# 96 short groups of unread TensorE products, at many operand distances, run behind the last product of an encoder kernel

## The chip, the cores and the metric

The kernel runs on one core of one Trainium2 chip. A core has TensorE (PE in the profile; PEld is its weight load), VectorE (DVE), ScalarE (ACT), GpSimd (POOL) and SyncE (SP), which work side by side and wait for each other through semaphores. A product reads two operands from SBUF, the stationary one (128 columns, loaded into the array first) and the moving one (256 or 512 columns streamed through it), and writes PSUM. The metric is the device time of one execution in microseconds, as a median over runs.

## The reference, cut to what matters

Two layers of an encoder on 256 tokens of width 2048, all in float32:

```
for i in range(DEPTH):                       # DEPTH = 2
    n = rms_norm(h, attn_norm[i])
    z = n @ w_in[i]                          # q, k, v and a query into 256 memory tokens
    h = h + concat([mix, cross]) @ w_o[i]    # neighbourhood attention in layer 0, grouped-query in layer 1
    n = rms_norm(h, mlp_norm[i])
    h = h + square(relu(n @ w_up[i])) @ w_down[i]   # 2048 -> 8192 -> 2048
return rms_norm(h, final_norm)
```

## The kernel before, in words

**Products.** Each float32 matrix is split into a rounded part and its remainder (`split`, lines 300 to 303: ScalarE makes "hi", VectorE "lo"), and each product is done as three TensorE products, hi by hi, hi by lo and lo by hi (`s_products` 216, `m_products` 203, `u_products` 729, `run` in `down_grains` 842). Where the weights stand still, 256 token columns move past them (lines 222 to 224 and 735 to 737); where the activations stand still, 512 weight columns move (lines 210 to 214 and 849 to 851). Attention has products of 256 columns too (365 to 367, 415 to 417).

**Stages.** The weights come chunk by chunk by DMA into rings of buffers; "grains" (class `Grain`, line 67) each load, split and multiply a half chunk, and `run_all` (247) goes through their list, starting loads and splits some grains ahead. The order is memory keys and values, layer 0 attention, output projection, MLP, then the same for layer 1. The MLP's down projection works by parts in a seven-product scheme (p1 to p7, `FIRST`, `SECOND`), whose shared sums stand in the tiles z0 and z1 and are folded into h (`folded`, 890), and its last part is done plainly (`plain_grains`, 903) in four column blocks of 512, 48 products each.

**The end.** The last block is done for one half of the tokens and then for the other. Line 945 runs the 24 products of a half and `finish` (1002) follows each half:

```
for i in range(NT):
    for n, (c, hf, k0, nk) in enumerate(PIECES):
        m_products(w, k0, nk, i, *own[c, hf], n == 0, n == 3, keep_order=True)
    w.done(w, i)
```

`finish` adds the scaled sum to h on VectorE (1006), sums squares on ScalarE (625, through `sum_squares`), reduces them on VectorE (1009, 309), takes the power on GpSimd (311), scales the row block on VectorE and ScalarE (1011, 1015, 1017) and starts four output transfers, two from ScalarE's queue and two from SyncE's (1020).

**Memory and order.** SBUF pools are stacked: "const", "keep" and "small" lie below, then "mlp" during the MLP, with z0 and z1 (8 KB a partition each), two buffers "c" (4 KB), six "a" (7 KB; the stationary activations of the down projection, line 794 and 800), and the split weights bh, bl, th, tl (their buffers serve h_p and l_p in the plain part). "side" lies at the other end. A pool that opens where another was closed waits tile by tile for what lies under it. Some operands are placed at offsets within their buffers, in bytes: `MOVING_AT` = 160, `STILL_AT` = 64 and the 480 in `wide("nT0", 480)` (lines 42 to 44, 185 to 187, 455 to 457, 739 to 741).

What one engine does comes in the order in which a planner found it ready, not in the order of the text, unless it is pinned. `pin` (line 189) keeps an instruction behind everything that the text has put on its engine so far. PSUM sums come from the pool "ps_acc", four buffers taken in turn; the last column block uses two of them.

Of the kernel before, what the change touches and what calls it, by code (L numbers as in the profile page):

```python
# [10 lines left out]
F32 = mybir.dt.float32  # L11
F32R = mybir.dt.float32r
# [5 lines left out]
P = 128  # L18
# [56 lines left out]
def encoder_kernel(ctx: ExitStack, tc: tile.TileContext, t: dict, out: bass.AP):  # L75
    nc = tc.nc
# [3 lines left out]
    def opened(name, side="left", space=None, bufs=1):  # L80
        kw = {"space": space} if space else {}
        manager = tc.tile_pool(name=name, bufs=bufs, side=side, reuse_waits="tile", **kw)
        pools[name] = manager, manager.__enter__()
        return pools[name][1]

    def closed(*names):
        for name in names:
            pools.pop(name)[0].__exit__(None, None, None)
# [57 lines left out]
    def halves_of(w):  # L146

        tiles = {}

        def load():  # L150
            tiles["raw"] = loaded(w.src, "U")

        def prep_early(hf):
            tiles[hf] = half_of_side(tiles["raw"], hf, MOVING_AT)

        def prep(hf):
            if hf == 0:
                tiles["raw"] = at.ring.tile([P, CH], F32, tag="raw", bufs=3, name="raw")
                nc.sync.dma_start(tiles["raw"], w.src)
            tiles[hf] = new_half(w.kind)  # L160
            split(*tiles[hf], tiles["raw"][:, hf * HALF : (hf + 1) * HALF])

        def run(hf):
            if hf == 0:
                w.start(w)
            hi, lo = tiles.pop(hf)
            if w.kind == "S":
                s_products(w, hf * (KT // 2), KT // 2, hi, lo)
            else:
                for i in range(NT):  # L170
                    m_products(w, w.first + 2 * hf, 2, i, hi, lo, w.begins and hf == 0, w.last and hf == 1)

        def after():
            if w.last:
                w.done(w)
            if w.early == "last":
                to_work()

        if w.early:
            return [Grain(lambda: run(0), None, load, None, lambda: prep_early(0), SOON),  # L180
                    Grain(lambda: run(1), after, None, None, lambda: prep_early(1), SOON)]
        return [Grain(lambda: run(0), None, None, None, lambda: prep(0)),
                Grain(lambda: run(1), after, None, None, lambda: prep(1))]
# [5 lines left out]
    pin = tc.keep_in_program_order  # L189

    def later(n, fn, *args):
        pending.append((state["tick"] + n, fn, args))

    def tick():
        state["tick"] += 1
        while True:
            due = [x for x in pending if x[0] <= state["tick"]]
            if not due:
                return
            pending.remove(due[0])  # L200
            due[0][1](*due[0][2])
# [24 lines left out]
    def begin():  # L226

        box["memT"] = at.cat.tile([P, KT, 512], F32R, tag="cat", name="memT")
        tiles = {}
        for w in plan[:FIRST_CHUNKS]:  # L230
            w.start(w)
        for q in range(4):
            for k in range(4 * q, 4 * q + 4):
                split_pair(box["memT"], mem0[:, k * SEQ : (k + 1) * SEQ], G_MEM, k)
                if k % 4 == 0:
                    for c, w in enumerate(plan[:FIRST_CHUNKS]):
                        if q % 2 == 0:
                            tiles[c] = new_half("S")
                        s = slice(q % 2 * 512, q % 2 * 512 + 512)
                        split(*(x[:, s] for x in tiles[c]), raws[c][:, q * 512 : (q + 1) * 512])  # L240
            for c, w in enumerate(plan[:FIRST_CHUNKS]):
                s = slice(q % 2 * 512, q % 2 * 512 + 512)
                s_products(w, 4 * q, 4, *(x[:, s] for x in tiles[c]))
        for w in plan[:FIRST_CHUNKS]:
            w.done(w)

    def run_all():
        begin()
        for w in plan[FIRST_CHUNKS:]:
            order.extend([w] if isinstance(w, Grain) else halves_of(w))  # L250
        reached = [0, 0, 0]

        def ahead(n):

            for stage in range(3):
                while reached[stage] < len(order) and reached[stage] < n + order[reached[stage]].ahead[stage]:
                    fn = order[reached[stage]].stages[stage]
                    reached[stage] += 1
                    if fn:
                        fn()  # L260

        for i in range(4):
            tick()
            ahead(min(i - 2, 0))
        for n, g in enumerate(order):
            ahead(n)
            g.run()
            if g.after:
                g.after()
            tick()  # L270
# [687 lines left out]
    def add_mlp(layer):  # L958
        for m in range(PK):
            plan.extend(up_grains(layer, 0, m))  # L960
        for x, (p, n) in enumerate(STEPS_OF):
            begins = x == 0 or HALF_OF[x - 1] != HALF_OF[x]
            ends = x == len(STEPS_OF) - 1 or HALF_OF[x + 1] != HALF_OF[x]
            up, down = up_grains(layer, p + 1, n), down_grains(layer, p, n, begins, ends)
            plan.extend((up[0], down[0], up[1], down[1]))
        for nb in range(4):
            plan.extend(plain_grains(layer, nb))
# [169 lines left out]
    add_o(1)  # L1137
    add_mlp(1)


    for j in range(8):
        later(3 + j, mem_squares, j)
# [4 lines left out]
        later(24 + j, x_norm, j)  # L1147
    later(26, x_stats)
    run_all()
    assert not pending, pending  # L1150
    closed(*reversed(list(pools)))

# [117 lines left out]
```

## Time and profile before

| what | us |
|---|---|
| median of two runs | 2051.15 |
| runs | 2050.47 and 2051.83 |
| the profiled execution, whole | 2048.73 |
| its span, first to last instruction | 2046.9 |
| TensorE busy | 2024.6 |
| VectorE busy | 1666.9 |
| ScalarE busy | 1242.6 |
| GpSimd busy | 126.4 |
| data read from HBM, in all | 401.32 MB, 200 GB/s over the span |

How to read it: times are counted from the first instruction. A line of the timeline has the start in us, the length in us, the engine, the line of the kernel, the operation, output and inputs by their names, the shapes, and how many records were merged; in brackets stands idle time just before it and what ended it. A line of the stretches has, for each engine, busy time and in brackets the records, then the granted TensorE clock, the share of the DMA engines and GB/s. A line of the groups has the count behind the x, then busy time in all and the mean of one in ns, then idle time and its releasers. A record of a product covers its whole way through the array, so records overlap; what a product takes from TensorE is the distance between two starts.

### The profile page before, as it was taken

How to read it: one execution, taken by the hardware profiler on the slowest of the kernel's cores; microseconds unless marked ns; L12 is line 12 of the kernel's file. 1: busy time of each engine (PE TensorE's matmuls, PEld its weight loads, DVE VectorE, ACT ScalarE, POOL GpSimd, SP SyncE). 2: the span in 40 equal slices, each digit the busy share in tenths (PEclk: the TensorE clock that was granted, in tenths of full speed). 3: DMA queues.
4: the chain of work that ended last, by engine and by line, in shares of the span. 5: the costliest groups of instructions: out<-in, count | busy, mean ns of one | idle time of the engine just before them, and what ended most of it. 6: DMA issues, size and time to landing. Idle time of an engine off the chain costs nothing.

```text
span 2046.9 us, 32742 instructions
## 1 busy us (share of the span) xinstructions
PE 2024.6 (99%) x13044; PEld 1832.8 (90%) x13044; DVE 1666.9 (81%) x2049; ACT 1242.6 (61%) x1628; POOL 126.4 (6%) x156
## 2 busy tenths in 40 slices
PE   8999999999999999999999999999999999999998
PEld 7899999889999999999988888889999999999996
DVE  6767677558998999989897667657989999999896
ACT  6645555456666666666656557556666666666664
POOL 0000000000000000010000001000000000000100
PEclk9999999999999999999999999999999999999999
DMA  7756666727777787777765544536777787777873
GB/s 281 281 193 208 217 211 213 288 77 237 228 229 232 217 241 230 221 233 231 225 211 216 178 170 146 200 114 229 233 231 231 220 240 217 232 226 221 243 222 131
DMA packets 101306, 440.16 MB, mean 215 GB/s; under 512 B 11424, under 2 KB 19232, under 8 KB 68000
## 3 DMA queue, kind: packets, MB, share of 16 engines
q1 hardware_dynamic: 82800, 402.40, 58.1%
q0 software_dynamic: 17776, 34.61, 9.1%
q8 instruction: 102, 1.67, 0.3%
q10 hardware_dynamic: 576, 1.05, 0.1%
q14 instruction: 52, 0.43, 0.1%
HBM read 401.32 MB, written 7.34 MB: 200 GB/s over the span
## 4 chain that ended last, share of the span: by engine, by line
PE 97%; DVE 1%; ACT 1%; issue 0%; DMA 0%; SPq 0%; POOLq 0%; POOL 0%; ACTq 0%
PE ps_u L737 11%; PE ps_u L735 11%; PE ps_u L736 11%; PE p L849 9%; PE p L850 9%; PE p L851 9%; PE ps_m L210 8%; PE ps_m L213 8%; PE ps_m L214 8%; PE ps_s L222 3%; PE ps_s L224 3%; PE ps_s L223 3%; PE pt_n L320 1%; DMA raw<-in_w_km 0%; PE pt_a L407 0%
## 5 line engine op out<-in xcount | busy, mean ns | idle before, releaser
L737 PE MATMUL ps_u<-hT,ul 128*128 128x256 f32 x2048 | 568.5, 278 | 1.8 <-DVE ul L303 1.8
L735 PE MATMUL ps_u<-hT,uh 128*128 128x256 f32 x2048 | 568.7, 278 | 0.0
L736 PE MATMUL ps_u<-hT,uh 128*128 128x256 f32 x2048 | 568.0, 278 | 0.0
L302 ACT ACTIVATE uh<-raw_U 128x1024 fp32r<-128x1024 f32 x278 | 294.7, 1061 | 313.9 <-PE ps_u L736 293.0
L735 PEld LDWEIGHTS ps_u<-hT,uh 128*128 128x128 f32 x2048 | 384.9, 188 | 5.5 <-ACT uh L302 0.3
L736 PEld LDWEIGHTS ps_u<-hT,uh 128*128 128x128 f32 x2048 | 384.8, 188 | 4.6
L737 PEld LDWEIGHTS ps_u<-hT,ul 128*128 128x128 f32 x2048 | 385.6, 188 | 3.7 <-DVE ul L303 2.6
L303 DVE TENSOR_TENSOR lo<-raw,hi 128x1024 fp32r<-128x1024 f32 (+1 forms) x224 | 266.3, 1194 | 148.0 <-ACT hi L302 145.9
L303 DVE TENSOR_TENSOR ul<-raw_U,uh 128x1024 fp32r<-128x1024 f32 x278 | 337.7, 1219 | 41.8 <-ACT uh L302 41.7
L302 ACT ACTIVATE hi<-raw 128x1024 fp32r<-128x1024 f32 (+1 forms) x224 | 231.7, 1040 | 204.4 <-PE ps_m L214 112.5
L302 ACT ACTIVATE th<-t 128x2048 fp32r<-128x2048 f32 x112 | 215.1, 1921 | 123.7 <-PE p L851 121.5
L303 DVE TENSOR_TENSOR tl<-t,th 128x2048 fp32r<-128x2048 f32 x112 | 256.2, 2287 | 36.5 <-ACT th L302 36.1
L303 DVE TENSOR_TENSOR bl<-b,bh 128x1536 fp32r<-128x1536 f32 x112 | 196.1, 1751 | 0.3 <-ACT bh L302 0.3
L850 PE MATMUL p<-tl,a_s 128*128 128x512 f32 x448 | 177.2, 395 | 0.0
L851 PE MATMUL p<-th,a_s 128*128 128x512 f32 x448 | 174.4, 389 | 0.0
L302 ACT ACTIVATE bh<-b 128x1536 fp32r<-128x1536 f32 x112 | 166.2, 1484 | 10.0 <-PE p L851 4.0
L829 POOL DMA_DIRECT2D t<-b x112 | 96.4, 861 | 1165.1 <-DVE t L828 506.7
L849 PE MATMUL p<-th,a_s 128*128 128x512 f32 x448 | 166.1, 395 | 0.0
L851 PE MATMUL p<-bh,a_s 128*128 128x512 f32 x336 | 131.1, 390 | 0.0
L850 PE MATMUL p<-bl,a_s 128*128 128x512 f32 x336 | 130.9, 390 | 0.0
L224 PE MATMUL ps_s<-nT,lo 128*128 128x256 f32 x448 | 125.4, 280 | 0.0
L222 PE MATMUL ps_s<-nT,hi 128*128 128x256 f32 x448 | 125.2, 279 | 0.0
(237 smaller groups left out, 3771.1 us busy)
## 6 DMA issues: line engine op xcount, KB each, us to landing
raw_U<-in_w_up SPq DMA_DIRECT2D x128, 1024.0 KB, 6.4
b<-in_w_pair SPq DMA_DIRECT2D x112, 768.0 KB, 4.5
raw<-in_w_o SPq DMA_DIRECT2D x32, 1024.0 KB, 5.0
t<-in_w_pair SPq DMA_DIRECT2D x112, 256.0 KB, 3.3
t<-b POOLq DMA_DIRECT2D x112, 256.0 KB, 6.8
raw<-in_w_b SPq DMA_DIRECT2D x21, 1024.0 KB, 5.0
raw<-in_w_av SPq DMA_DIRECT2D x12, 1024.0 KB, 5.0
raw<-in_w_aq SPq DMA_DIRECT2D x12, 1024.0 KB, 5.0
```

Of the source, the lines that this page charges most:

```text
L210: first = nc.tensor.matmul(w.ps[i], ah, hi[:, s], start=st, stop=False)
L213: nc.tensor.matmul(w.ps[i], ah, lo[:, s], start=False, stop=False)
L222: nc.tensor.matmul(ps, hi[:, s], acts[:, k, :SEQ], start=k == 0, stop=False)
L224: nc.tensor.matmul(ps, lo[:, s], acts[:, k, :SEQ], start=False, stop=k == KT - 1)
L302: first = nc.scalar.activation(dst_hi, src, AF.Copy)
L303: return first, nc.vector.tensor_tensor(dst_lo, src, dst_hi.bitcast(F32), op=ALU.subtract)
L735: nc.tensor.matmul(ps, hi[:, s], acts[:, k, :SEQ], start=k == 0, stop=False)
L736: nc.tensor.matmul(ps, hi[:, s], acts[:, k, SEQ:], start=False, stop=False)
L737: nc.tensor.matmul(ps, lo[:, s], acts[:, k, :SEQ], start=False, stop=k == KT - 1)
L849: nc.tensor.matmul(ps, a[:, 0, ai, :], hi[:, s], start=begins, stop=False)
L850: nc.tensor.matmul(ps, a[:, 0, ai, :], lo[:, s], start=False, stop=False)
L851: nc.tensor.matmul(ps, a[:, 1, ai, :], hi[:, s], start=False, stop=ends)
```

## The change

A function `unread_products` is added after line 1138 and called right after `run_all()`, so that its instructions come behind the whole program in the text. It closes the pool "mlp" and opens "idle" in its place, with two tiles that are filled with ones: "small_room" (640 columns, by GpSimd) and "room" (9344 columns, by VectorE). It takes one PSUM buffer of the pool "ps_acc", into which all its products go; nothing reads it. Every product is pinned.

First come 60 products of 512 columns from "small_room". Then 64 groups `narrow(x, e)`: two products of 512 columns, then fifteen of 256, in threes with the pattern of lines 735 to 737. Then 32 groups `wide_ones(y, z)`: two products of 256 columns, then twelve of 512, in threes with the pattern of lines 849 to 851. `piece` shifts an operand by `place % 256` bytes within "room", in steps of 32 bytes. As weights are loaded one product ahead, the distance that counts here is from a moving operand to the next stationary one: in a narrow group it is x inside, and e from the last entry product to the first of the fifteen; in a wide group y inside and z at the entry. That is eight distances inside, and eight (narrow) or four (wide) at the entry.

```diff
+    def unread_products():
+
+        closed("mlp")
+        idle = opened("idle")
+        small_room = idle.tile([P, 640], F32R, name="small_room")
+        nc.gpsimd.memset(small_room.bitcast(F32), 1.0)
+        room = idle.tile([P, 9344], F32R, name="room")
+        nc.vector.memset(room.bitcast(F32), 1.0)
+        ps = at.acc.tile([P, 512], F32, tag="acc", name="ps_x")
+
+        def product(still, moving, start, stop):
+            n = moving.shape[-1]
+            pin(nc.tensor.matmul(ps[:, :n], still, moving, start=start, stop=stop))
+
+        for n in range(60):
+            product(small_room[:, 512:640], small_room[:, :512], n == 0, n == 59)
+
+        def piece(first, place, n):
+            first += place % 256 // 4
+            return room[:, first : first + n]
+
+        def features(k, lo):
+            return piece(512 * k + 256 * lo, 0, 256)
+
+        def narrow(x, e):
+            for n in range(2):
+                product(piece(7424, 0, P), piece(4096 + 512 * n, x - e, 512), n == 0, n == 1)
+            for k in range(5):
+                hi, lo = (piece(f + 128 * k, x, P) for f in (2560, 3328))
+                product(hi, features(k, 0), k == 0, False)
+                product(hi, features(k, 1), False, False)
+                product(lo, features(k, 0), False, k == 4)
+
+        def wide_ones(y, z):
+            for n in range(2):
+                product(piece(2560, y, P), features(n, 0), n == 0, n == 1)
+            for k in range(4):
+                hi, lo = (piece(f + 128 * k, z, P) for f in (7424, 8320))
+                bh, bl = (piece(f + 512 * (k % 3), z - y, 512) for f in (4096, 5760))
+                product(hi, bh, k == 0, False)
+                product(hi, bl, False, False)
+                product(lo, bh, False, k == 3)
+
+        for x in range(0, 256, 32):
+            for e in range(0, 256, 32):
+                narrow(x, e)
+        for y in range(0, 256, 32):
+            for z in range(0, 256, 64):
+                wide_ones(y, z)
...
     run_all()
+    unread_products()
```

## The prediction, made before the change was run

> **What bounds the kernel now.** I read the page first, for the span and for whether anything but TensorE could carry the end.
>
> ```profile
> span 2046.9 us, 32742 instructions
> PE 2024.6 (99%) x13044; PEld 1832.8 (90%) x13044; DVE 1666.9 (81%) x2049; ACT 1242.6 (61%) x1628; POOL 126.4 (6%) x156
> PEclk9999999999999999999999999999999999999999
> ...
> PE 97%; DVE 1%; ACT 1%; issue 0%; DMA 0%; SPq 0%; POOLq 0%; POOL 0%; ACTq 0%
> ```
>
> TensorE is busy 99% of the span and makes 97% of the chain that ended last, at the full granted clock. So products that are added to its stream add their own time, unless they can be placed where TensorE stands still. The next view is the end of the run in order of time, because the change puts its work there: TensorE, then VectorE, then the other engines and the output.
>
> ```profile
> 2036.80 0.39 PE L213 MATMUL ps_m<-l_p,a_p 128*128 128x512 f32 x1
> ...
> 2037.70 0.39 PE L214 MATMUL ps_m<-h_p,a_p 128*128 128x512 f32 x1
> 2038.13 0.75 DVE L1006 SCALAR_TENSOR_TENSOR h<-ps_m,inv,h 128x512 f32<-128x512 f32 x1 [1.66 <-PE ps_m L214]
> 2040.09 0.55 POOL L311 TENSOR_TENSOR fin_r<-fin_v,mhalf 128x1 f32<-128x1 f32 x1 [4.80 <-DVE fin_v L309]
> 2041.35 0.48 DVE L1015 TENSOR_SCALAR h<-h,fin_r 128x512 f32<-128x512 f32 x1
> 2041.43 0.95 ACTq L1020 DMA_DIRECT2D out<-h  x2
> 2041.46 0.81 SPq L1020 DMA_DIRECT2D out<-h  x2
> ```
>
> The last product starts at 2037.70. Everything behind it, the final normalisation and the output transfers, takes until 2046.9. TensorE is therefore free for 9.2 us at the end and nowhere else.
>
> **How fast a product follows the one before.** The record of a product (0.28 us at 256 columns, 0.39 at 512) holds its passage through the array and overlaps the next, so the price is the distance from start to start. I took it from four stretches of the timeline. The rows are the first and the last of each.
>
> ```profile
> 136.41 0.28 PE L415 MATMUL av<-pT,vm 128*128 128x256 f32 x1
> ...
> 137.49 0.28 PE L365 MATMUL sc_ps<-km,qmT 128*128 128x256 f32 x1
> ...
> 952.22 0.28 PE L737 MATMUL ps_u<-hT,ul 128*128 128x256 f32 x1
> ...
> 957.52 0.28 PE L737 MATMUL ps_u<-hT,ul 128*128 128x256 f32 x1
> ...
> 1003.62 0.28 PE L735 MATMUL ps_u<-hT,uh 128*128 128x256 f32 x1
> ...
> 1004.22 0.28 PE L737 MATMUL ps_u<-hT,ul 128*128 128x256 f32 x1
> 1004.33 0.28 PE L735 MATMUL ps_u<-hT,uh 128*128 128x256 f32 x1
> ...
> 1008.98 0.28 PE L737 MATMUL ps_u<-hT,ul 128*128 128x256 f32 x1
> 1009.10 0.40 PE L849 MATMUL p<-th,a_s 128*128 128x512 f32 x1
> 1009.33 0.40 PE L850 MATMUL p<-tl,a_s 128*128 128x512 f32 x1
> 1009.57 0.39 PE L851 MATMUL p<-th,a_s 128*128 128x512 f32 x1
> ...
> 1011.88 0.39 PE L849 MATMUL p<-bh,a_s 128*128 128x512 f32 x1
> ```
>
> At 256 columns there are two steady rates for the same product with nothing else changed: 41 steps in 1008.98 - 1004.33 = 4.65 us, or 113.3 ns, and 45 steps in 957.52 - 952.22 = 5.30 us, or 117.8 ns. After a change of product the quick stretch first pays: five steps in 1004.22 - 1003.62 = 0.60 us, or 120 ns each. A short group, the nine steps from 136.41 to 137.49, never becomes quick: 1.08 us, or 120 ns each. At 512 columns, the four steps from 2036.80 to 2037.70 give 226 to 227 ns, which is twice 113.3 = 226.7; the twelve from 1009.10 to 1011.88 give 2.78 us, or 231.7 ns, with a worst single step of 0.24 us (1009.33 to 1009.57). No row is quicker than 113.3 and 226.7 at the full clock. So the place of the operands, or how a group was entered, costs 0 to 13 ns a product. The profile has no addresses, so I can't price each distance of the change by itself, only bound all of them by these rows.
>
> **The change, part by part.** It removes nothing and moves nothing; no DMA is issued, so no queue of SP, ACT or POOL gets longer by a transfer.
>
> Pool and buffers. The pool "mlp" is closed and "idle" opened at its start. Its 2.5 and 36.5 KB a partition lie over z0, z1, both c and the first two and a little of the third of the six buffers "a", by the sizes in the code. z0 was last read in the fold, 192 products of line 210 to 214 earlier; the "a" buffers are read by the last products.
>
> The two memsets. GpSimd fills 640 columns. The nearest rows are its own fills at the start:
>
> ```profile
> L130 POOL MEMSET ones<- 128x128 f32 x1 | 0.2, 205 | 0.3 <-POOLq L1260 0.3
> L132 POOL MEMSET mhalf<- 128x8 f32 x1 | 0.1, 105 | 0.0
> ...
> POOL fin_r L311 <- DVE fin_v L309: 61.5, 2, 56.7
> ```
>
> They give 100 ns for 120 more columns, so 640 columns take about 0.63 us. GpSimd waits idle for 56.7 us ahead of the first L311, and z0 is free by then, so I take nothing for it. If it is queued behind the second L311 (end 2040.64), TensorE would start at 2041.3 and not 2037.93: 3.3 us. Nothing that matters stands behind it on GpSimd but that L311.
>
> VectorE fills 9344 columns. The row L1015 (0.48 us for 512 columns) scaled up gives 8.8 us, L1006 (0.75 us) gives 13.7; without a fixed part it could be half of the first. It must wait for the readers of its part of "a" (the last of them six products ahead of the end), and what is queued behind it on VectorE is the final normalisation, so the output transfers may be 9 us later; their cover is 240 us of products. Its own cover is the first 60 products, 13.6 us from 2037.93, so until 2051.5. Even behind the whole normalisation (end 2041.83) it is done at 2050.6. At 13.7 us it would be 4.0 us late. I take nothing, which is the nearest row's answer.
>
> The products. 60 + 64 x 17 + 32 x 14 = 1596, of which 64 x 15 + 32 x 2 = 1024 have 256 columns and 60 + 64 x 2 + 32 x 12 = 572 have 512. They are pinned one behind the other and behind the last real product, they write one PSUM bank in order, and nothing reads it, so no wait lies between them. Quick bound: 1024 x 113.3 + 572 x 226.7 = 116.05 + 129.65 = 245.7 us. Dear bound: 1024 x 124 (the worst single step inside that 0.60 us, if the other four took 119) + 512 x 240 + 60 x 226.7 = 263.5 us. What I take: at 256 columns the groups have fifteen products, so a group that becomes quick still pays its first five, (5 x 120 + 10 x 113.3) / 15 = 115.5; a slow one 117.8; one like the short group 120. The middle is 117.8: 120.6 us. At 512, the groups have twelve; half of them at 226.7 and half at 231.7 is 229.2: 512 x 229.2 = 117.35 us. The 60 of the first stretch have the operands at equal places, as in a row with one rate all through, so 226.7: 13.6 us. Sum 251.55 us.
>
> The Trainium skill ("TensorE: Matmul & The Clock Gate", section "Step-by-step: what each phase is for") says that TensorE reads weights and the moving operand through two independent SBUF ports, so that loading the next weights takes nothing from the running product. By it distances would cost nothing and the sum would be the quick one; the 113.3 and 117.8 above, for one kind of product, speak against it. Section "Back-to-back issue gap" of the same page has N / 2.4 + 2.5 ns, 109.2 and 215.8; by that the products would take an estimated 235.2 us; the rows above, at 113.3 and 226.7, disagree.
>
> The end. The last record starts one step ahead of the sum's end: 2037.70 + 0.23 + 251.55 - 0.23 = 2289.25, and ends 0.39 later, 2289.64. Then the end of the program. In before, the last transfers are issued by 2042.4 and land 3.0 to 3.2 us after their issue, which leaves 1.3 to 1.8 us to 2046.9:
>
> ```profile
> out<-h ACTq DMA_DIRECT2D x4, 256.0 KB, 3.2
> out<-h SPq DMA_DIRECT2D x4, 256.0 KB, 3.0
> ```
>
> Part of this is the checking of those landings, which is over long before; I take 1.2. Span 2290.8. The execution lasted 2048.73, 1.83 beyond its span, so 2292.7; the median of the runs, 2051.15, is 2.42 above the profiled one, so a median of 2295.1, which I forecast as 2295.0 us: +11.9%.
>
> **The rivals.** (1) Distances cost nothing: all at the quick rate. For it, most long stretches are quick; against it, the groups here are short and their entries change on purpose. 251.55 falls to 245.7: 2289.
>
> (2) Some distance is cheaper than any in before, so that the quick rate isn't the floor. At the very start, at half the clock, a step is 0.213 us:
>
> ```profile
> 6.39 0.58 PE L222 MATMUL ps_s<-memT,hi 128*128 128x256 f32 x1 [6.39 <-ACT hi L302]
> ...
> 7.68 0.41 PE L224 MATMUL ps_s<-memT,lo 128*128 128x256 f32 x1
> ...
> 10.88 0.37 PE L224 MATMUL ps_s<-memT,lo 128*128 128x256 f32 x1
> 11.09 0.28 PE L222 MATMUL ps_s<-memT,hi 128*128 128x256 f32 x1
> ```
>
> Fifteen steps in 3.20 us, half of which is 106.7 ns. All 2168 units of 256 columns at 106.7 would be 231.3 us: 2275. Against it: no step in before comes near. (By the gap formula of the Trainium skill, on the page "TensorE: Matmul & The Clock Gate", named above, it would be an estimated 2279.)
>
> (3) Some distances clash worse than any in before. Price up to the dear bound: 263.5, so 2307. For it: before has few distances, fixed in its code; against it: the clashes that it has end within five steps or stay at 5 ns.
>
> (4) TensorE stands still at the entry, for one of the two fills: 3.3 or 4.0 us, or both late.
>
> ```profile
> 2038.10:2042.00 3.90, 0.00 (x0) 0.00 (x0) 2.21 (x5) 2.04 (x4) 0.55 (x1) 1.00 0.40 150
> 2042.00:2046.90 4.90, 0.00 (x0) 0.00 (x0) 0.00 (x0) 0.02 (x1) 0.00 (x0) 0.50 0.56 214
> ```
>
> The granted clock falls to 0.50 about 3.9 us after the last product, so a wait of that length may also be followed by cold steps: the start ran cold from 6.39 to 11.09, 4.7 us, a loss of half of it, 2.4 us. Together 3 to 10 us, middle 5: 2300. Against it: the fills have 56.7 us of idle GpSimd and 13.6 us of products as cover.
>
> (5) The other side: not slower. The products have no reader; if they are left out of the program, or fall into the 9.2 us that TensorE is free at the end, the time stays 2051. Only about 40 of the 1596 fit there, since 9.2 us / 0.2267 is 40, so the point from which it decides is that they aren't issued at all. Against it: they are written as ordinary products into a held bank.
>
> **How the numbers follow.** Chances: the forecast 0.62, rival 1 0.12, rival 2 0.02, rival 3 0.12, rival 4 0.09, rival 5 0.03. The range goes from 2287 (rival 1 at the profiled execution's level, 2289.2 - 2.42) to 2307 (the dear bound) and holds the forecast, rivals 1 and 4 and half of 3. About 2% is what a measurement of this kernel can tell from no change, and every case but rival 5 lies over 10% above before: slower 0.97, same 0.03, faster 0.
>
> **What would show it right or wrong.** Right: 14640 products; the first added one follows the one at 2037.70 by 0.23 us; the added ones take 246 to 263 us with no idle time between; within a group of fifteen, starts lie 113 to 124 ns apart, and within one of twelve 226 to 240, differing from group to group; the output transfers end early, and the span ends 1 to 2 us behind the last product. Wrong: a gap behind the 60 products or ahead of them (rival 4), steps over 130 ns at 256 columns for whole groups (rival 3 and beyond my range), all steps alike (rival 1), steps under 113 (rival 2).

## The result, and the profile after

The change takes 2297.32 us, the median of two runs (2294.45 and 2300.19), against 2051.15: the ratio is 1.12, with a 95% interval from 1.1138 to 1.1262. Forecast were 2295.0 us, 2287 to 2307. The profiled execution is the longer of the two runs, 2300.19 us.

The page of the changed kernel, its head and its chain:

```profile
span 2298.4 us, 35936 instructions
...
PE 2280.7 (99%) x14640; PEld 2062.5 (90%) x14640; DVE 1674.1 (73%) x2050; ACT 1243.2 (54%) x1628; POOL 127.1 (6%) x157
...
PE ps_x L1152 11%; PE ps_u L737 9%; PE ps_u L735 9%; PE ps_u L736 9%; PE p L849 7%; PE p L850 7%; PE ps_m L210 7%; PE p L851 7%; PE ps_m L213 7%; PE ps_m L214 7%; PE ps_s L224 3%; PE ps_s L222 3%; PE ps_s L223 3%; DMA t<-in_w_pair 1%; DVE ul L303 1%
```

TensorE has 1596 products more and 256 us more of busy time; VectorE has gained 7.2 us, and ScalarE and GpSimd less than 1. The chain that ended last now closes with the added line, L1152, at 11%. The same place as before, the end of the real work, in order of time over TensorE, GpSimd and VectorE:

```profile
2043.68 0.39 PE L214 MATMUL ps_m<-h_p,a_p 128*128 128x512 f32 x1
2043.91 0.84 PE L1152 MATMUL ps_x<-small_room 128*128 128x512 f32 x3
...
2041.23 0.63 POOL L1145 MEMSET small_room<- 128x640 f32 x1
...
2044.11 0.75 DVE L1006 SCALAR_TENSOR_TENSOR h<-ps_m,inv,h 128x512 f32<-128x512 f32 x1 [1.65 <-PE ps_m L214]
2046.76 7.84 DVE L1147 MEMSET room<- 128x9344 f32 x1 [1.90 <-issue]
2054.52 0.10 DVE L1009 TENSOR_REDUCE ss_f<-ssq 128x1 f32<-128x4 f32 x1
```

The first added product follows the last real one by 0.23 us. The small fill ended at 2041.86, 2.05 us ahead of its need. The large one ended at 2054.60, 2.9 us ahead of the end of the 60 products at 2057.51, and it did push the final normalisation back (L1009 behind it), under the products. The three stretches of the added part (busy time and records by engine, then the granted clock):

```profile
2043.90:2057.50 13.60, 13.60 (x61) 11.26 (x60) 9.92 (x6) 2.06 (x4) 0.56 (x1) 1.00 0.16 61
2057.50:2200.60 143.10, 143.10 (x1089) 137.42 (x1088) 0.00 (x0) 0.00 (x0) 0.00 (x0) 1.00 0.02 7
2200.60:2297.50 96.90, 96.86 (x450) 79.54 (x448) 0.00 (x0) 0.00 (x0) 0.00 (x0) 1.00 0.00 1
```

TensorE is busy without a gap at the full clock: 13.6 us for the 60, 143.1 for the narrow groups, 96.7 for the wide ones with the last step (to 2297.07 + 0.23), 253.4 in all. Five groups, cut to their inner products and merged in a line each (start, length in all, records), show that their steps differ:

```profile
2096.45 1.41 PE L1152 MATMUL ps_x<-room 128*128 128x256 f32 x11
...
2109.65 1.46 PE L1152 MATMUL ps_x<-room 128*128 128x256 f32 x11
...
2154.56 1.48 PE L1152 MATMUL ps_x<-room 128*128 128x256 f32 x11
...
2204.31 2.21 PE L1152 MATMUL ps_x<-room 128*128 128x512 f32 x9
...
2267.58 2.51 PE L1152 MATMUL ps_x<-room 128*128 128x512 f32 x10
```

Less the last record's 0.28 or 0.39 us, over one step less than records: narrow (64, 32) 113 ns, (64, 224) 118, (160, 96) 120; wide (0, 64) 227, (160, 128) 236. The first two have their operands at the same places and differ by the entry alone.

### The profile page after: what moved, and what is told of

It is laid out like the page before. It is cut to its first block, busy times and chain, and to the rows that moved or that the text cites. A ratio compares the mean times of both kernels' runs of the same rounds, so it can differ in the third digit from the quotient of the medians.

```text
span 2298.4 us, 35936 instructions
## 1 busy us (share of the span) xinstructions
PE 2280.7 (99%) x14640; PEld 2062.5 (90%) x14640; DVE 1674.1 (73%) x2050; ACT 1243.2 (54%) x1628; POOL 127.1 (6%) x157
## 4 chain that ended last, share of the span: by engine, by line
PE 94%; DVE 3%; DMA 2%; issue 1%; ACT 1%; SPq 0%; DVEq 0%; ACTq 0%
PE ps_x L1152 11%; PE ps_u L737 9%; PE ps_u L735 9%; PE ps_u L736 9%; PE p L849 7%; PE p L850 7%; PE ps_m L210 7%; PE p L851 7%; PE ps_m L213 7%; PE ps_m L214 7%; PE ps_s L224 3%; PE ps_s L222 3%; PE ps_s L223 3%; DMA t<-in_w_pair 1%; DVE ul L303 1%
## 5 line engine op out<-in xcount | busy, mean ns | idle before, releaser
L1152 PE MATMUL ps_x<-room 128*128 128x256 f32 (+1 forms) x1536 | 239.9, 318 | 0.0
L1152 PEld LDWEIGHTS ps_x<-room 128*128 128x128 f32 x1536 | 217.2, 188 | 22.6
```

What stands on the lines that cost most here:

```text
L1152: pin(nc.tensor.matmul(ps[:, :n], still, moving, start=start, stop=stop))
```

## The experiments

**The change again, beside the kernel before.** Ahead of the added part the first profiled execution was 6 us later than the one of before (2043.68 against 2037.70 for the last real product).

> The change unaltered, beside runs of the kernel before on one chip. Theory (the added products take 253.2 us, as they did in the first profile, and of that first profile's time some 6 us were waits for transfers ahead of the added part): the added stretch is 253.2 us again to 0.1, the last real product starts near 2037 and not at 2043.7, and the time is 2293 to 2295 us. Rival (the waits ahead belong to the change): the last real product starts near 2043 again, and the time is 2297 to 2300 us.

Measured: 2293.57 us, ratio 1.119 (1.1175 to 1.1206). In its timeline the last real product starts earlier than in before:

```profile
2036.82 0.39 PE L214 MATMUL ps_m<-h_p,a_p 128*128 128x512 f32 x1
2037.05 0.39 PE L1152 MATMUL ps_x<-small_room 128*128 128x512 f32 x1
```

The view of the tile of the added sums has the first and the last start of the groups:

```profile
L1152 PE MATMUL ps_x<-room x1536: 274/282/406, 2050.7 to 2290.2; 128*128 128x256 f32 x128, 128*128 128x512 f32 x64
```

The added stretch, from the first added start to the last, is 253.16 us in both executions, and none of its steps differs by more than 1 ns. The 6 us belong to that one execution, not to the change: set product against product, it fell behind the second execution by 3.6 us in its first 72 us and by another 3.3 between 1870 and 1993 us, ahead of every added product. The theory holds in its times; what the lost time was spent on was not looked into.

**Quick places.** 

```diff
-                narrow(x, e)
+                narrow(64, 32)
...
-                wide_ones(y, z)
+                wide_ones(0, 64)
```

> All 64 narrow groups at distance 64 inside and 32 at the entry, all 32 wide ones at 0 and 64, so as many products of each width as in the change. Theory (the distance from a moving operand to the next stationary one sets the step): the added stretch, first added start to last, falls from 253.2 to 247.9 us (64 groups of 2.174 us and 32 of 2.975 us, as this pair of distances took in the change, and 13.6 us), the time by 5 us. Rival (distances cost nothing and the steps differ by where in the stream a group lies): 253 us, no change.

**Dear places.** The same with `narrow(160, 96)` and `wide_ones(160, 128)`.

> All narrow groups at 160 inside and 96 at the entry, all wide ones at 160 and 128. Theory: the added stretch rises to 255.5 us (64 groups of 2.252 us, 32 of 3.055 us, and 13.6 us), 7.6 us above the run with the quick places. Rival (distances cost nothing): 253 us, the same as the run with the quick places.

Measured, side by side: 2287.46 us (ratio 1.1164, 1.1147 to 1.118) and 2295.75 us (1.1204, 1.1187 to 1.1221), with as many products of each width. The same view, first with the quick places and then with the dear ones:

```profile
L1152 PE MATMUL ps_x<-room x1536: 276/276/399, 2050.3 to 2284.1; 128*128 128x256 f32 x128, 128*128 128x512 f32 x64
```

```profile
L1152 PE MATMUL ps_x<-room x1536: 276/283/403, 2050.6 to 2292.1; 128*128 128x256 f32 x128, 128*128 128x512 f32 x64
```

233.8 against 241.5 us, and with the 60 products 247.3 and 255.1 where 247.9 and 255.5 were expected. The places, inside and at the entry together, are worth 8 us; that distances cost nothing is refuted, and so is the rival that the steps go by where in the stream a group lies.

**No cover.** 

```diff
-        for n in range(60):
-            product(small_room[:, 512:640], small_room[:, :512], n == 0, n == 59)
+        for n in range(1):
+            product(small_room[:, 512:640], small_room[:, :512], True, True)
```

> 59 of the first 60 products left out, 13.4 us of product time. Theory (the fill of the large tile, 7.84 us on VectorE and over 10.9 us behind the last real product's start, is hidden by these 60 products alone): TensorE stands still for about 10.5 us ahead of the first narrow group, the granted clock falls to half on the way, and the cold start costs 2 to 3 us more, so the time stays within 2 us of the change. Rival (the fill does not hold TensorE up, or can start earlier): the time falls by 13 us.

Measured: 2292.97 us (ratio 1.1189, 1.117 to 1.1207), 244.3 above its runs of before, as the change again is 244.2 above its own. TensorE and VectorE in order of time:

```profile
2038.96 0.39 PE L1152 MATMUL ps_x<-small_room 128*128 128x512 f32 x1
2049.71 1.22 PE L1152 MATMUL ps_x<-room 128*128 128x512 f32 x2 [10.36 <-DVE ss_f L1009]
...
2041.81 7.84 DVE L1147 MEMSET room<- 128x9344 f32 x1 [1.90 <-issue]
```

The stretch in which TensorE waits, and the narrow groups:

```profile
2039.40:2049.60 10.20, 0.00 (x0) 0.00 (x0) 8.30 (x3) 0.72 (x2) 0.00 (x0) 0.71 0.12 47
2049.70:2194.70 145.00, 144.99 (x1088) 139.21 (x1089) 1.30 (x3) 1.34 (x2) 0.55 (x1) 0.99 0.02 8
```

13.4 us of products are gone, and TensorE waits 10.4 us for the fill (the profile names VectorE's next instruction; the fill, which ends at 2049.65, is the one read). The clock falls on the way, and the narrow groups take 145.1 in place of 143.1 us, all of the difference in the first of them. The theory holds: the 60 products were the cover of the fill, and cost almost nothing.

**Which pair of operands clashes.** 

```diff
+        for nxt in range(0, 256, 32):
+            for own in range(0, 256, 32):
+                for n in range(48):
+                    s = n * (nxt - own)
+                    product(piece(7424, s, P), piece(512 * (n % 4), s - own, 256), n == 0, n == 47)
```

> In place of the groups, 64 groups of 48 products of 256 columns, for each of eight distances from a moving operand to the next stationary one and each of eight distances from a moving operand to its own stationary one, both by steps of 32 bytes. Theory (the clash is between the next weight load and the running product): the step is about 113.5 to 114 ns wherever the next distance is 64, for all own distances, and 117 to 120 ns at the other next distances. Rival (own distance): 113.5 where the own distance is 64. Rival (neither, the entry decides): quick and slow groups are spread without a pattern. Expected stretch 64 x 48 steps of 118 ns, 362 us.

Measured: a stretch of 362.2 us, and only two of the 64 pairs quick, (64, 64) and (192, 192). Four of them, next and own distance (64, 64), (64, 0), (160, 64) and (192, 192):

```profile
2154.13 4.81 PE L1152 MATMUL ps_x<-room 128*128 128x256 f32 x41
...
2142.78 5.02 PE L1152 MATMUL ps_x<-room 128*128 128x256 f32 x41
...
2290.20 5.16 PE L1152 MATMUL ps_x<-room 128*128 128x256 f32 x41
...
2358.24 4.81 PE L1152 MATMUL ps_x<-room 128*128 128x256 f32 x41
```

That is 113, 118.5, 122 and 113 ns. With a next distance of 64 the other seven own distances give 115.9 to 118.6, with an own distance of 64 the other next ones 116.6 to 122.5. The theory that the next distance alone decides fell, and so did the rival of the own distance. Both quick pairs have equal distances, so that the operands keep their places within 256 bytes from product to product; but the other six such pairs are not quick (116.7 to 120.1 ns), so that is not enough. Whether the entry decides, the second rival, this run could not tell.

**Shifted.**

```diff
+        for x in (64, 160, 0, 32):
+            for shift in range(0, 256, 32):
+                for n in range(48):
+                    product(piece(7424, shift + x, P), piece(512 * (n % 4), shift, 256), n == 0, n == 47)
```

> In place of the groups, 32 groups of 48 products of 256 columns: distances 64, 160, 0 and 32, each with both operands shifted together by 0, 32, ... 224 bytes. Theory (only the distance counts): the step is one value per distance at all eight shifts, near 114, 119.5, 119.5 and 118 ns. Rival (the operand's own place in a stretch of 256 bytes counts): it differs by more than 2 ns among the shifts.

Measured: at 160, 0 and 32 one value each at all eight shifts, within 0.2 ns (119.9 to 120.1, 119.9 to 120.0, 118.3 to 118.4). At 64 the groups take turns, 117.8, 113.3, 117.8, 113.3 and so on. The theory holds for three distances; for the fourth the rival, the place, could not be told from the entry.

**The order of shifts.** Distance 64 alone.

```diff
+        for shift in (0, 64, 128, 192, 32, 96, 160, 224, 0, 0, 0, 0, 32, 32, 32, 32):
+            for n in range(48):
+                product(piece(7424, shift + 64, P), piece(512 * (n % 4), shift, 256), n == 0, n == 47)
+        for shift in (0, 0, 0, 0, 32, 32, 32, 32):
+            for n in range(2):
+                product(piece(7424, 0, P), piece(4096 + 512 * n, shift + 32, 512), n == 0, n == 1)
+            for n in range(48):
+                product(piece(7424, shift + 64, P), piece(512 * (n % 4), shift, 256), n == 0, n == 47)
```

> Distance 64 alone, in 24 groups of 48 products of 256 columns, with both operands shifted by 0, 64, 128, 192, 32, 96, 160, 224, then four times 0 and four times 32 without a break in the addresses, then the same eight with two products of 512 columns ahead of each group. Theory (two steady rates at one distance, 113.3 and 117.8 ns, and the entry decides): groups at one and the same shift are found at both rates, and the continued groups keep the rate they have. Rival (the place decides): shifts 0, 64, 128 and 192 all at 117.8, the other four all at 113.3, in every order.

Four groups at the shifts 0, 0, 32, 32, the first, tenth, fifth and thirteenth of the run:

```profile
2051.61 5.70 PE L1152 MATMUL ps_x<-room 128*128 128x256 f32 x47
...
2101.73 5.26 PE L1152 MATMUL ps_x<-room 128*128 128x256 f32 x45
...
2074.07 5.26 PE L1152 MATMUL ps_x<-room 128*128 128x256 f32 x45
...
2118.07 5.46 PE L1152 MATMUL ps_x<-room 128*128 128x256 f32 x45
```

118 and 113 ns at shift 0, 113 and 118 at shift 32: the same places are found at both rates. Groups that go on without a break keep theirs (four at shift 0 at 113.3, four at 32 at 117.8). So the place is refuted, and what ran ahead of a group is left, as the theory has it. The last four groups of the run narrow it further. Each is shift 32 behind the same two products of 512 columns, and their rates are 113.3, 117.8, 113.3 and 117.8 ns. Stretches of the second and the third of them:

```profile
2171.39 4.87 PE L1152 MATMUL ps_x<-room 128*128 128x256 f32 x40
...
2177.63 4.58 PE L1152 MATMUL ps_x<-room 128*128 128x256 f32 x39
```

The second, third and fourth follow a group with the same code and the same places as their own. So the places at the entry don't decide alone either. What does, be it carried over from further back or not tied to places at all, these runs don't show.

**Widths and fewer weights.** Two runs, each in place of the groups.

```diff
+        for cols in (128, 256, 384, 512):
+            for x in range(0, 256, 32):
+                for n in range(36):
+                    product(piece(7424, x, P), piece(512 * (n % 4), 0, cols), n == 0, n == 35)
```

```diff
+        for w in (128, 64, 32):
+            for x in range(0, 256, 32):
+                for n in range(36):
+                    pin(nc.tensor.matmul(ps[:w, :256], piece(7424, x, w), piece(512 * (n % 4), 0, 256),
+                                         start=n == 0, stop=n == 35))
```

> In place of the groups, 32 groups of 36 products with 128, 256, 384 and 512 moving columns at eight distances. Theory (the price is per weight load, of 128 columns each, so it doesn't grow with the moving columns): over 113.3 ns per 256 columns, 0 to 1 ns at distance 64 and 4 to 8 ns at the others, at 256, 384 and 512 alike; at 128 columns the load itself may set the step. Rival (the price is per moving column): at 512 twice that of 256, 8 to 13 ns.

> In place of the groups, 24 groups of 36 products of 256 columns with 128, 64 and 32 stationary columns at eight distances. Theory (the weight load's reads clash with the running product's): the price over 113.3 ns, 4 to 6 ns at all distances but 64 with 128 stationary columns, falls to about half with 64 and a quarter with 32. Rival (the price is paid once a product whatever is loaded): it stays at 4 to 6 ns.

The first run, at 256 columns and distance 64, and at 512 and distances 0 and 160; then the second, at distance 160, with 128, 64 and 32 stationary columns:

```profile
2094.45 3.58 PE L1152 MATMUL ps_x<-room 128*128 128x256 f32 x29
...
2171.34 6.51 PE L1152 MATMUL ps_x<-room 128*128 128x512 f32 x28
...
2213.14 6.69 PE L1152 MATMUL ps_x<-room 128*128 128x512 f32 x28
```

```profile
2073.84 3.64 PE L1186 MATMUL ps_x<-room 128*128 128x256 f32 x29
...
2107.63 3.59 PE L1186 MATMUL ps_x<-room 128*64 128x256 f32 x29
...
2141.09 3.57 PE L1186 MATMUL ps_x<-room 128*32 128x256 f32 x29
```

The first lines read 118, 226.7 and 233.3 ns. Over the product's own 113.3 for each 256 columns, the eight distances cost 4.0 to 6.7 ns at 256, 3.3 to 6.7 at 384 and 0 to 7.6 at 512: a price per product, not per moving column. That distance 64 is the cheap one, which the theory also had, did not hold: it costs 4.5 ns at 256 and 6.7 at 512, and at 512 the cheap ones are 0 and 192. The second three read 120, 118.2 and 117.5 ns, so with a quarter of the stationary columns 2.5 of 6.7 ns are saved there. Other distances behave differently: at distance 0 the three steps are 120.0, 113.3 and 117.7, at 224 they are 117.8, 119.1 and 117.4. Over all eight the mean price is 5.1, 3.7 and 2.5 ns, not the half and the quarter of the theory, and not unchanged either: both fell as they were stated. At 128 moving columns all distances take 111.6 to 111.7 ns, nearly the step of 256.

**The floor of the load.** As the second of these, with 64 and 128 moving columns.

```diff
+        for cols in (64, 128):
+            for w in (128, 64, 32):
+                for x in (0, 64, 160, 224):
+                    for n in range(36):
+                        pin(nc.tensor.matmul(ps[:w, :cols], piece(7424, x, w), piece(512 * (n % 4), 0, cols),
...
```

> 24 groups of 36 products with 64 and 128 moving columns and 128, 64 and 32 stationary columns, at distances 0, 64, 160 and 224. Theory (a load of 128 stationary columns takes some 107 to 111 ns by itself and so sets the step of narrow products): with 128 stationary columns the step is 111.6 ns at both 64 and 128 moving columns; with 64 it falls to about 56 to 62 ns, and with 32 to the product's own 57 ns at 128 moving columns and about half at 64. Rival (a fixed time per product, whatever is loaded): 111.6 ns in all groups.

At 128 moving columns the step is 111.7 ns with 128 stationary columns, 60.0 with 64 and 60.0 with 32. A group with 128 and one with 64 (less the last record's 0.27 and 0.22 us):

```profile
2101.84 3.40 PE L1187 MATMUL ps_x<-room 128*128 128x128 f32 x29
...
2117.78 1.91 PE L1187 MATMUL ps_x<-room 128*64 128x128 f32 x29
```

So a load of 128 columns sets that step, as the theory has it, and the product's own is 60, not 57. At 64 moving columns the step is 111.7 at first and then the clock is halved, though TensorE's records leave no gap:

```profile
2052.00:2055.70 3.70, 3.70 (x36) 1.00 0.27 103
2060.00:2066.00 6.00, 6.00 (x30) 0.50 0.00 0
2077.00:2088.00 11.00, 11.00 (x106) 0.50 0.01 1
2091.70:2093.90 2.20, 2.20 (x46) 0.50 0.00 0
2094.00:2097.00 3.00, 3.00 (x99) 1.00 0.02 5
2098.00:2113.00 15.00, 15.00 (x136) 1.00 0.00 1
```

All but the last stretch have 64 moving columns: the first two with 128 stationary ones (steps of 111.7 and then 213.3 ns), the third with 64 (106.7), the next two with 32 (53.3 and then 32). The last has 128 of both. The clock fell 5.6 us after the first of these groups began and came back at 2093.9, within the groups of 64 moving and 32 stationary columns, not with the wider products behind them.

**The real kernel's own groups.** If the entry decides, the kernel before could be helped: its first down group after each up group (the tiles th and tl) runs at 231.7 ns. The pool of the MLP was moved by 96 and by 32 bytes, without the change.

```diff
                 at.mlp = opened("mlp")
+                at.mlp.tile([P, 24], F32, name="pad")
...
-                own[c, hf] = half_of_side(own[0], hf, MOVING_AT)
+                own[c, hf] = half_of_side(own[0], hf, MOVING_AT + 96)
```

> The kernel before, without the change, with everything in the pool of the MLP moved by 96 bytes, so that the distance from the last moving operand of an up group to the first stationary one of the down group becomes 64 instead of 224; the distances inside stay 64 and 0. Theory (the entry decides which of two rates a group runs at): the first down group, twelve products at 231.7 ns now, runs nearer 227, 0.03 to 0.06 us each for some 110 groups, so 3 to 7 us less. Rival (the rate of that group comes from its own operands): no change beyond 1 us.

> The kernel before, with the pool of the MLP moved by 32 bytes: from up to down the distance becomes 0, from down to up 64. Theory (entry): the five slow first products of an up group, 32 ns in all, fall away, 3 us over some 100 groups, if 64 is a quick entry; the down groups may become quicker or stay. Rival (no effect of the entry): no change beyond 1 us.

Measured: 2057.99 us, ratio 1.0043 (1.0029 to 1.0056), and 2062.19 us, 1.0062 (1.005 to 1.0075), against 2049.35. Neither is a gain. The bounds of one up group and the two down groups behind it, moved by 96 and then by 32 (the added line makes line 849 of before line 850 here):

```profile
996.50 0.28 PE L735 MATMUL ps_u<-hT,uh 128*128 128x256 f32 x1
...
1002.03 0.28 PE L737 MATMUL ps_u<-hT,ul 128*128 128x256 f32 x1
1002.15 0.39 PE L850 MATMUL p<-th,a_s 128*128 128x512 f32 x1
...
1004.87 0.39 PE L850 MATMUL p<-bh,a_s 128*128 128x512 f32 x1
```

```profile
998.63 0.28 PE L735 MATMUL ps_u<-hT,uh 128*128 128x256 f32 x1
...
1004.16 0.28 PE L737 MATMUL ps_u<-hT,ul 128*128 128x256 f32 x1
1004.28 0.40 PE L850 MATMUL p<-th,a_s 128*128 128x512 f32 x1
...
1007.03 0.39 PE L850 MATMUL p<-bh,a_s 128*128 128x512 f32 x1
```

Moved by 96, the twelve products of the down group take 2.72 us, 226.7 ns each, as the theory expected; from each first start to the start behind the group, that is 6.3 us less over all down groups. But the up group's 47 steps take 5.53 us, 117.7 ns, all through, where they had become quick after five: 14.4 us more over all up groups. Its entry had gone from 96 to 0 at the same time, and the expectation did not price that. Moved by 32, up groups lose 17.2 us and down groups gain 3.7, so the gain that the theory expected from an entry at 64 did not come. These sums, 8.1 and 13.5 us, are nearly all of what the last real product starts later than in before (7.8 and 13.4). Both rivals are refuted: the up groups kept their operands where they were, and what runs ahead of them changed their rate. With 64 and 0 inside, the two entries always add up to 64, so one can't be moved without the other; the other five positions were not tried, and no version that beats the kernel before was found.

## Why the prediction was right

**The place and the cover.** Right: no gap at the entry (0.23 us), the fills hidden. The small fill took the 0.63 us that were forecast, but not in the 56.7 us of idle GpSimd that were its cover: it came behind the first L311 and used 0.63 of the idle time between the two, 2.05 us ahead of its need. The large one took 7.84 us where L1015's row gave 8.8, and had 2.9 us to spare. The prediction had no term for the 1.9 us ahead of it on VectorE, and the cover took them.

**The products.** Forecast 251.55 us, measured 253.4. The 60 took 13.6 as forecast. The narrow groups' inner steps average 118.0 ns where 117.8 was taken. The term that was mis-sized is that of 512 columns: half of them quick was the assumption (229.2 ns), and inside the wide groups the steps average 232.2. By what each product takes to the next start, the 512 of that width in the groups took 118.9 us for 117.35, and the 1024 of 256 columns 120.9 for 120.6. A likely reason shows in the run with the widths: of eight distances only 0 and 192 have steps under 232 ns there, and the rows of before that the term was taken from have their operands, by its code, at distance 0 inside a group.

**The dear bound.** It stood at 263.5 us; the dear pairs, used throughout, give 255.1 + 0.2. Single groups were dearer than these (2.267 us for a narrow one of the change against 2.252), so this is no upper end. The quick bound of 245.7 was not reached either: 247.3 + 0.2 with the quick places, most of it because each group still pays for its entry (in a narrow one 471 ns for the two products of 512 columns, where 453 is the quick rate).

**The rivals.** That distances cost nothing is refuted by the quick and dear places, 8 us apart. The Trainium skill says that loading the next weights takes no read bandwidth from the running product ("TensorE: Matmul & The Clock Gate", section "Step-by-step: what each phase is for"). What the prediction drew from it, the quick sum, does not hold here: 113.3 and 120 ns are found for one kind of product at two pairs of places. Whether the ports themselves are the cause, no run shows. No step of 256 columns in a steady group, in any run at the full clock, was under 113.3, so a cheaper distance was not found; a dearer pair than in the steady rows of before exists (122 ns, with places that wander from product to product), but no narrow group of the change was as dear inside (119.9 at most). The wait at the entry did not occur. Without the cover it is 10.4 us and 2 us of half clock, but that is not the case that the 3 to 10 us were given to: with the 60 products in place the fill would have to end 2.9 us later before TensorE waits at all. The products ran in full, so the other side was out.

**The end.** 1.2 us were taken; the span ends 2298.4 - 2297.07 - 0.39 = 0.94 us behind the last record. What that time is spent on, the checking of landings or something else, no run shows. The difference of 2.4 us between the profiled execution and the median of before was carried over as a term of its own; the change again, at 2293.57, is 1.4 us below the forecast.

**What was luck.** The path and the cover were right and the products 0.7% too cheap, but that the time came as near as it did is in part luck. In the run again the median lies 0.24 us above the profiled execution, not 2.42, so that term was 2.2 us too large; the products were 1.85 us too small; the two nearly cancel. The first median, 2297.32, stands above the forecast because one of its two executions had lost some 6 us before the added part began.

What stays open is the mechanism under the two rates. It is neither the next distance alone, which the description of the change takes to be the one that counts, nor the own one; at distance 64 it is not the place within 256 bytes, and the price does not follow the length of the load in proportion. What runs ahead of a group changes its rate, as the up groups of the kernel moved by 96 bytes show, but the places at its entry are not enough to tell which rate follows, and no rule was found that does.

## What to carry to other kernels

Price added TensorE work by the distance between starts in the stage that it joins, and look for two rates of one and the same product before taking a mean: here they differ by 4%, and the one that a group falls into can come from what ran ahead of it. An offset that helps one kind of group changes the entry of the next, so both have to be counted. And the long fill of a buffer cost nothing here while other products kept TensorE running, but 10.4 us and a fall of the clock when they didn't.

## What the runs showed of the hardware that was not expected

A product of 128 moving columns takes 111.7 ns, almost as long as one of 256 at 113.3, and with 64 stationary columns it falls to 60.0, so the load of 128 columns sets it (the output rows fall along with the stationary columns, and the two were not varied apart). The records of the loads agree in their differences: 189, 134 and 108 ns on average with 128, 64 and 32 columns in the run with fewer weights, about 0.84 ns a column, an estimated 108 ns for 128. The Trainium skill has a load at its columns over 1.2, in the section "LDWEIGHTS (loading the stationary operand)" of the page named above, an estimated 106.7 ns, near the 111.7 here.

The granted clock fell to 0.50 in a stretch where TensorE's records leave no idle time, with 64 moving columns at a step of 111.7 ns, and came back while the moving columns were still 64, once 32 stationary columns let the step fall to 53.3 ns at half the clock. A busy share of 100% did not keep the clock up. An estimate of how full the array was: if 64 columns take those 53.3 ns, they fill a quarter of the steps of 213.3, half of those of 106.7, in both of which the clock stayed at half, and all of the last, which brought it back. That the clock goes by this share was not tested on its own.

VectorE stood 1.9 us ahead of the large fill in every profile shown, waiting for nothing that the profile names; the cause was not looked into.
